# Two decoder layers on one core: weight parts moved into the common pool of slices, latent scores as three rounded products, c loaded as one row

## The chip, the core and the metric

The kernel runs on one core of one Trainium2 chip. The time is the device time in microseconds (us) of one launch. Engines: PE is TensorE (matrix products and transposes), ACT is ScalarE, DVE is VectorE, POOL is GpSimd, SP is SyncE, which here issues all transfers. SBUF is the on-chip memory of 128 partitions, PSUM the accumulators that PE writes, in banks of 128x512 fp32.

## The reference

One sequence of 512 tokens of width 1024 passes two layers of three sub-layers each. Every sub-layer is wrapped alike, and the six inner functions are, in order: feed-forward, latent attention, feed-forward, feed-forward, dilated attention, feed-forward.

```python
def sandwich(x, fn, pre_g, post_g, shift, scale, gate, res_w):
    hn = rmsnorm(x, pre_g) * (1 + scale[:, None, :]) + shift[:, None, :]
    y = rmsnorm(fn(hn), post_g)
    return x + res_w * gate[:, None, :] * y

def swiglu(h, w_gate, w_up, w_down):
    return (jax.nn.silu(h @ w_gate) * (h @ w_up)) @ w_down
```

shift, scale and gate are rows of `silu(c) @ w_mod[i] + b_mod[i]`, with c one row of 1024 numbers. Latent attention (16 heads) projects h to 384 query and 256 key-value numbers and a shared rotary key of 32, normalizes them, expands them to queries and keys of 64 + 32 and values of 64 per head, and takes causal softmax attention. Dilated attention (16 heads of 64) projects h to nine blocks (query, key and value for three dilations), scores each query against a window of keys with a bias, and mixes the three results by their log-sums. All data is fp32; D_MODEL is 1024 and D_FF 2816.

## The kernel before

**Products.** A dense product is `mm3` (L141 to L146): both operands are held as a rounded part and a rest, in the type fp32r, and three products are summed in one bank: high by high (L143), high by low (L144) and low by high (L145). For w the two operand pairs are `w[0]`, `w[1]`; either the weights or the activations stand on the side that is loaded into the array. The scores of latent attention are the exception: one fp32 product of 96 rows (L847), for block i of 128 queries against the n = (i + 1)·128 columns of keys that the mask can leave, so 128, 256, 384 or 512.

**Weights.** `weights` (L123) fetches a 128x1024 block (512 KB) into a slot of the tag `raw` (RAW = 5 slots, L120), ACT writes its high part in one instruction (L128, tag `whi`), and DVE writes the low part in two halves (L130, tag `wlo`). `whi` and `wlo` have SLOTS = 6 slots of their own in the pool `ring`. Only the first two weights after each change of sub-layer are taken by `weights_sliced` and the class `Sliced` (L53 to L75, splits in L68 and L72): their parts lie in slices of 128x512.

**Slices.** The pool `sl` has SLICES = 44 slots of 128x512, all with the tag `s` (method `s`). From it come h, the partial sums y, the feed-forward's products g in two parts, latents, queries, keys, values, the dilated projections and their outputs, tables and biases. The slots of one tag are handed out in the order in which the program asks for them: the k-th request takes the slot that the request 44 before it leaves. Where an instruction lies in an engine's queue is set when the program is built, by a scheduler that keeps to such orders; on the chip each engine runs its queue strictly in order.

**Feed-forward** (`Ffn`). D_FF is cut into 22 units of 128, in groups of 5, 6, 5 and 6 (GROUPS). Of a unit, `gate_up_mm` sums 48 products of 128x512, 24 in a gate bank and 24 in an up bank, from two 128x1024 weights. `gate_up_out` (L540 to L557) then takes silu of the gate bank (ACT, L552), times the up bank (DVE, L554), the high part of the result g (ACT, L555) and its low part (DVE, L557). After a group, `down` multiplies g with the group's `w_down` blocks (one 128x1024 weight for each unit) in four tiles of 128 tokens and two halves of 512 columns, and `y_part` adds the bank to y. The last group's down products are the sub-layer's tail; during it the next sub-layer's input is normalized, transposed (`turn`) and modulated, and its first units are taken in halves of 256 tokens (`head`: three units of a feed-forward, six tiles of an attention). The first feed-forward starts four units together (START) in `start`, while x arrives.

**Latent attention** (`Mla`, from L685). After six tiles of `mla_in`, `rest` projects keys (`key`), queries (`query`), rotary queries (`rope`) and values (`value`), each when the table BESIDE says so, beside the attention of 8 pairs of heads in four blocks each (`attend`: scores on PE, masking and minimum on DVE L850, exp on ACT L853, transposes L875, products with the values).

**Dilated attention** (`Dil`, from L928). For each of 8 pairs of heads nine tiles are projected (`tile`: one 128x1024 weight, 24 products, a copy on ACT at L1040). Beside the tiles n = 0 to 8 of the next pair run the present pair's parts: at n = 0 to 3 the scores (PE L1075, DVE L1088), after the last of them `tops` (DVE L1120, L1121), which passes minima through DRAM by several transfers; at n = 4 `exps`, 24 exponentials on ACT (L1140) whose sums go through DRAM again (`norm`, L1159), then `norm_out` (DVE L1167 to L1169), which sends 1/sum through DRAM (L1170, L1173); at n = 6 to 8 transposes (L1195), copies (L1199) and products with the values (L1220).

**Start** (`start`, from L322). c is broadcast to 128 partitions by a transfer of 512 KB into `cs` (L379), silu is applied in place, and the rows of x are normalized (`rise`) and transposed (L370). `mod_fold` multiplies a 128x1024 block of `w_mod` with cs and sums each partition (DVE L165), then adds the bias (L168).

Of the kernel before, what the change touches and what calls it, by code (L numbers as in the profile page):

```python
# [14 lines left out]
P = 128  # L15
# [10 lines left out]
SLICES = 44  # L26
SLOTS = 6
# [16 lines left out]
class Halves:  # L44
    def __init__(self, parts):
        self.parts = [x.rearrange("p (k c) -> p k c", c=P) for x in parts]
# [6 lines left out]
class Sliced:  # L53


    def __init__(self, t, src):
        self.t, self.src = t, src
        self.raw = t.ring.tile([P, CH], F32, tag="raw", name="raw", bufs=RAW)
        self.out = [[t.s(F32R), t.s(F32R)] for _ in range(2)]

    def at(self, j):
        return slice(j * SEQ, (j + 1) * SEQ)

    def fetch(self, j):
        self.t.nc.sync.dma_start(self.raw[:, self.at(j)], self.src[:, self.at(j)])

    def top(self, j):
        self.t.nc.scalar.activation(self.out[0][j], self.raw[:, self.at(j)], AF.Copy)  # L68

    def low(self, j):  # L70
        hi, lo = self.out
        self.t.nc.vector.tensor_tensor(lo[j], self.raw[:, self.at(j)], f(hi[j]), ALU.subtract)  # L72
# [5 lines left out]
class Trunk:  # L78
    def __init__(self, ctx, tc, a):
# [3 lines left out]
        self.ring = ctx.enter_context(tc.tile_pool(name="ring", bufs=SLOTS))  # L83
# [39 lines left out]
    def weights(self, src, flat=False):  # L123
        raw = self.load(src)
        n = src.shape[-1]
        hi = self.ring.tile([P, CH], F32R, tag="whi", name="whi")[:, :n]
        lo = self.ring.tile([P, CH], F32R, tag="wlo", name="wlo")[:, :n]
        self.nc.scalar.activation(hi, raw, AF.Copy)  # L128
        for r in (slice(0, n // 2), slice(n // 2, n)):
            self.nc.vector.tensor_tensor(lo[:, r], raw[:, r], f(hi[:, r]), ALU.subtract)  # L130
        return [t if flat else t.rearrange("p (k c) -> p k c", c=P) for t in (hi, lo)]

    def weights_sliced(self, src):
        w = Sliced(self, src)
        for j in range(2):
            w.fetch(j)
            w.top(j)
            w.low(j)
        return w.parts()
# [19 lines left out]
    def mod(self, l, n, k):  # L159
        self.mod_fold(l, n, k, self.load(self.a["w_mod"][l, n, k]))  # L160

    def mod_fold(self, l, n, k, raw):
# [5 lines left out]
        self.mod_out(l, n, k, t, lambda out, b: nc.vector.tensor_tensor(out, t[:, 0:1], b, ALU.add))  # L168
# [163 lines left out]
    def start(self, sub):  # L332
# [19 lines left out]
        def rise(i):  # L352
# [10 lines left out]
            r = self.scale_of(ss)  # L363
            nc.vector.tensor_scalar(t[0], x[0], r, None, ALU.mult)
# [14 lines left out]
        nc.sync.dma_start(self.cs, self.a["c"].broadcast_to([P, D]))  # L379
        stream(0)  # L380
        stream(1)
        nc.sync.dma_start(self.small, self.a["small"])
        raw = [self.load(self.a["w_mod"][*mods[0], 0])]
        stream(2)
        raw.append(self.load(self.a["w_mod"][*mods[1], 0]))
        stream(3)
        w = [Sliced(self, self.a["w_gu"][sub.l, sub.s, 0, g]) for g in range(2)]
        sub.w[0] = [x.parts() for x in w]
        for j in range(2):
            for x in w:  # L390
                x.fetch(j)
# [3 lines left out]
        with self.tc.manual_schedule(engines={ACT, DVE}):  # L395
            nc.scalar.activation(self.cs, self.cs, AF.Silu)
            self.new_h()
            rise(0)
            rise(1)
            self.mod_fold(*mods[0], 0, raw[0])  # L400
            rise(2)
            self.mod_fold(*mods[1], 0, raw[1])
# [11 lines left out]
            for x in w:  # L414
                x.top(1)
                x.low(1)
# [3 lines left out]
        for n, kind in sorted([(n, 1) for n in range(1, START)] + [(n, 0) for n in range(1, KT)]):  # L420
            if kind:
                sub.gate_up_load(n)
# [83 lines left out]
class Ffn:  # L506
# [11 lines left out]
    def gate_up_load(self, ft, sliced=False):  # L518
        t = self.t
        make = t.weights_sliced if sliced else t.weights  # L520
        self.w[ft] = [make(t.a["w_gu"][self.l, self.s, ft, g]) for g in range(2)]

    def prepare(self):
        self.gate_up_load(0, True)
# [39 lines left out]
    def products(self, b, q, i, d, js):  # L564
        m = GROUPS[q][1]
        for j in js:
# [3 lines left out]
                [x[:, d * SEQ : (d + 1) * SEQ] for x in self.wd[q][j]],  # L570
# [4 lines left out]
    def down(self, q, i):  # L575
# [3 lines left out]
        if q not in self.wd:  # L579
            self.wd[q] = [  # L580
                t.weights(t.a["w_down"][self.l, self.s, at + j], flat=True) for j in range(m)
# [49 lines left out]
class Mixer:  # L631
# [5 lines left out]
    def out_weights(self, j):  # L637
        t = self.t
        if j not in self.wo:
            self.wo[j] = t.weights(t.a[self.w_o][j], flat=True)  # L640

    def products(self, b, i, d, js):
        t = self.t
        for j in js:
# [4 lines left out]
                [x[:, d * SEQ : (d + 1) * SEQ] for x in self.wo[j]],  # L649
# [35 lines left out]
class Mla(Mixer):  # L685
# [37 lines left out]
    def prepare(self):  # L723
        self.w = {u: self.t.weights_sliced(self.t.a["mla_in"][u]) for u in range(2)}
# [31 lines left out]
    def value(self, j, e):  # L756
        t = self.t
        if not self.wv:
            self.wv += [t.weights(t.a["mla_v"][k], flat=True) for k in range(2)]
        b = t.bank()  # L760
        for k in range(2):
            ls = [x[:, j * P : (j + 1) * P] for x in self.latn[k]]
            t.mm3(b, ls, [x[:, e * SEQ : (e + 1) * SEQ] for x in self.wv[k]], k == 0, k == 1)
# [8 lines left out]

    def key(self, g, p):
        t, nc = self.t, self.t.nc
        b = self.project(self.weight(g, 0), 2 * p, (0, 1))
        k = self.k[2 * g + p] = [t.s() for _ in range(2)]
        nc.scalar.activation(k[0][0:64], b[0:64], AF.Copy)
        nc.vector.tensor_copy(k[1][0:64], b[64:128])
        for y in k:
            nc.gpsimd.tensor_scalar(y[64:96], self.lat[2][64:96], 1.0, 0.0, ALU.mult, ALU.add)  # L780

    def query(self, g, p):
        nc = self.t.nc
        b = self.project(self.weight(g, 1), 3 * p, (3, 4, 5))
# [616 lines left out]
```

## Time and profile before

| | us |
|---|---|
| median of 3 runs | 2277.34 |
| lowest, highest | 2276.07, 2277.81 |
| the profiled execution's own time | 2277.64 |
| its span in the trace | 2275.9 |
| PE busy | 2241.0 |
| DVE busy | 1203.6 |
| ACT busy | 861.4 |
| POOL busy | 106.1 |

The time of a run is the span plus about 1.7 us around it (2277.64 against 2275.9). A row of the profile names the line, engine, operation, output and input of a group of instructions. In a window's row stand its bounds, its length, the busy time of PE, weight loads, DVE, ACT and POOL with the number of instructions behind each, the clock granted to PE as a share of full speed, the share of busy DMA and GB/s. A row of the timeline has the start in us from the begin of the span, the time taken and, in brackets, the idle time of the engine before it and what ended that. Matrix products overlap: the distance between two starts is what one costs, and the printed duration includes the part that lies under the next.

### The profile page before, as it was taken

What the parts mean: (1) busy time and instruction counts of PE and PEld (TensorE: products, weight loads), DVE (VectorE), ACT (ScalarE), POOL (GpSimd) and SP (SyncE); (2) the same over time, 40 slices, a digit from 0 to 9 for tenths busy, and PEclk for the clock granted to TensorE, in tenths of its full rate; (3) what the DMA queues carried; (4) which work ended last, traced back from release to release, by engine and by line L of the source; (5) the groups of instructions that cost most, each with busy time, mean ns of one, the idle gap of its engine ahead of it and who ended that gap; (6) DMA issues with size and microseconds to landing.
All of it is one profiled execution on the core that took longest, in us unless ns stands there. A gap on an engine that the chain in (4) does not pass through costs nothing. (4 is left out here: it accounts for less than half of the span.)

```text
span 2275.9 us, 30179 instructions
## 1 busy us (share of the span) xinstructions
PE 2241.0 (98%) x11418; PEld 1853.5 (81%) x11418; DVE 1203.6 (53%) x2711; ACT 861.4 (38%) x1751; POOL 106.1 (5%) x143
## 2 busy tenths in 40 slices
PE   6999999999999999999999999999999999999998
PEld 5888888877898888898888888777878878888887
DVE  7666566677665366474554473344334367243344
ACT  4432135577633132353222352444344345332232
POOL 0000001210110000020000010000000002000000
PEclk9999999999999999999999999999999999999999
DMA  8575662211255365344653523333333332242231
GB/s 311 162 251 183 186 231 69 99 47 56 70 172 184 93 208 176 107 140 123 192 175 114 155 93 105 80 95 88 83 89 80 96 79 79 75 130 98 79 111 37
DMA packets 121366, 284.56 MB, mean 125 GB/s; under 512 B 44145, under 2 KB 48516, under 8 KB 121220
## 3 DMA queue, kind: packets, MB, share of 16 engines
q1 hardware_dynamic: 121220, 282.63, 40.5%
q8 instruction: 89, 1.46, 0.3%
q14 instruction: 57, 0.47, 0.1%
HBM read 280.19 MB, written 2.39 MB: 124 GB/s over the span
## 5 line engine op out<-in xcount | busy, mean ns | idle before, releaser
L143 PE MATMUL mm<-s,whi 128*128 128x512 f32 (+1 forms) x2116 | 797.8, 378 | 3.7 <-ACT whi L128 2.5
L144 PE MATMUL mm<-s,whi 128*128 128x512 f32 (+1 forms) x2116 | 792.2, 374 | 0.0
L145 PE MATMUL mm<-s,wlo 128*128 128x512 f32 (+1 forms) x2116 | 791.5, 374 | 0.0
L128 ACT ACTIVATE whi<-raw 128x1024 fp32r<-128x1024 f32 (+1 forms) x356 | 369.7, 1053 | 973.2 <-PE mm L144 441.8
L130 DVE TENSOR_TENSOR wlo<-raw,whi 128x512 fp32r<-128x512 f32 (+1 forms) x712 | 466.0, 693 | 409.9 <-ACT whi L128 401.7
L143 PEld LDWEIGHTS mm<-s,whi 128*128 128x128 f32 x2116 | 399.3, 189 | 84.4 <-issue 7.0
L145 PEld LDWEIGHTS mm<-s,wlo 128*128 128x128 f32 x2116 | 399.6, 189 | 70.9
L144 PEld LDWEIGHTS mm<-s,whi 128*128 128x128 f32 x2116 | 399.5, 189 | 67.8
L143 PE MATMUL mm<-whi,s 128*128 128x512 f32 x848 | 332.4, 392 | 2.0 <-ACT s L679 1.3
L144 PE MATMUL mm<-wlo,s 128*128 128x512 f32 x848 | 330.4, 390 | 0.0
L145 PE MATMUL mm<-whi,s 128*128 128x512 f32 x848 | 330.1, 389 | 0.0
L165 DVE CUSTOM_DVE_ANT_0 raw<-raw,cs 128x1024 f32<-128x1024 f32 x130 | 160.1, 1236 | 108.5 <-DMA raw<-w_mod 107.9
L143 PEld LDWEIGHTS mm<-whi,s 128*128 128x128 f32 x848 | 159.2, 188 | 36.6 <-issue 2.5
L145 PEld LDWEIGHTS mm<-whi,s 128*128 128x128 f32 x848 | 159.2, 188 | 33.4 <-issue 0.3
L144 PEld LDWEIGHTS mm<-wlo,s 128*128 128x128 f32 x848 | 159.2, 188 | 32.6 <-issue 0.3
L554 DVE TENSOR_TENSOR gg<-silu,mm 128x512 f32<-128x512 f32 (+1 forms) x95 | 60.4, 635 | 172.2 <-PE mm L145 168.8
L444 DVE TENSOR_TENSOR s<-mm,s 128x512 f32<-128x512 f32 x112 | 76.5, 689 | 124.8 <-PE mm L145 124.7
L314 POOL TENSOR_TENSOR mv<-mv,mhalf 128x1 f32<-128x1 f32 x48 | 35.9, 750 | 1498.9 <-DVE mv L313 1496.4
L555 ACT ACTIVATE s<-gg 128x512 fp32r<-128x512 f32 (+1 forms) x97 | 57.4, 591 | 53.3 <-DVE gg L554 53.2
L552 ACT ACTIVATE silu<-mm 128x512 f32<-128x512 f32 (+1 forms) x95 | 51.4, 543 | 30.6 <-PE mm L145 30.5
L1040 ACT ACTIVATE s<-mm 128x512 f32<-128x512 f32 (+3 forms) x156 | 46.2, 374 | 34.8 <-PE mm L145 34.8
L448 ACT ACTIVATE s<-mm 128x512 f32<-128x512 f32 x40 | 23.8, 595 | 85.8 <-PE mm L145 85.5
(165 smaller groups left out, 1738.1 us busy)
## 6 DMA issues: line engine op xcount, KB each, us to landing
raw<-w_gu SPq DMA_DIRECT2D x168, 512.0 KB, 4.4
raw<-w_mod SPq DMA_DIRECT2D x130, 512.0 KB, 4.7
raw<-w_down SPq DMA_DIRECT2D x88, 512.0 KB, 4.3
raw<-dil_in SPq DMA_DIRECT2D x70, 512.0 KB, 3.6
s<-w_mod SPq DMA_DIRECT2D x28, 256.0 KB, 6.6
raw<-w_gu SPq DMA_DIRECT2D x16, 256.0 KB, 3.2
raw<-mla_o SPq DMA_DIRECT2D x8, 512.0 KB, 4.7
raw<-dil_o SPq DMA_DIRECT2D x8, 512.0 KB, 3.7
```

The lines of the kernel that those rows point to most:

```text
L128: self.nc.scalar.activation(hi, raw, AF.Copy)
L130: self.nc.vector.tensor_tensor(lo[:, r], raw[:, r], f(hi[:, r]), ALU.subtract)
L143: mm(out, w[0], m[0], start=first, stop=False)
L144: mm(out, w[0], m[1], start=False, stop=False)
L145: mm(out, w[1], m[0], start=False, stop=last)
L165: nc.vector.tensor_tensor_reduce(raw, raw, self.cs, 1.0, 0.0, ALU.mult, ALU.add, accum_out=t[:, 0:1])
L314: nc.gpsimd.tensor_tensor(v[:, 1:2], v[:, 0:1], self.mhalf[:, 0:1], ALU.pow)
L444: nc.vector.tensor_tensor(y, b, y, ALU.add)
L552: nc.scalar.activation(s, banks[0], AF.Silu)
L554: nc.vector.tensor_tensor(v, s, banks[1], ALU.mult)
L555: nc.scalar.activation(ghi, v, AF.Copy)
L1040: nc.scalar.activation(out, src, AF.Copy)
```

## The change

**One pool for weights too.** SLOTS and the tags `whi` and `wlo` are gone; SLICES is 68 instead of 44, which takes the room that became free (6 slots of two 128x1024 parts are 24 slices). The class `Sliced` is now `Weights`, and every weight's parts are four slices of the tag `s` (two high, two low), requested when the program creates the weight. A high part is two instructions of 128x512 on ACT (now L75), the low part two on DVE (now L79). The raw block is still fetched by one transfer, of 512 KB, into one of 5 slots (now L68 in the list of transfers).

**Scores of latent attention.** Queries and keys are split into high and low parts (`part_rows`: three ACT and two DVE instructions of 64x512 on one bank), the shared rotary key and the rotary queries too (`turned_parts`, `rope`), and the scores are three fp32r products.

**Start.** c comes as one row of 4 KB, is spread over the partitions by two products with a row of ones, and silu reads it from PSUM. The two first blocks of `w_mod` are fetched ahead of the second and third tile of x, `small` after x. `mod_fold` is cut into `mod_dot` and `mod_sum`. The second halves of the first two weights are fetched and split later (at n == 2).

```diff
-SLICES = 44
-SLOTS = 6
+SLICES = 68
...
-class Sliced:
+class Weights:
     def __init__(self, t, src):
-        self.t, self.src = t, src
+        self.t, self.src, self.n = t, src, src.shape[-1]
         self.raw = t.ring.tile([P, CH], F32, tag="raw", name="raw", bufs=RAW)
         self.out = [[t.s(F32R), t.s(F32R)] for _ in range(2)]
...
     def top(self, j):
-        self.t.nc.scalar.activation(self.out[0][j], self.raw[:, self.at(j)], AF.Copy)
+        self.t.nc.scalar.activation(self.both(j)[0], self.raw[:, self.at(j)], AF.Copy)
     def low(self, j):
-        hi, lo = self.out
-        self.t.nc.vector.tensor_tensor(lo[j], self.raw[:, self.at(j)], f(hi[j]), ALU.subtract)
+        hi, lo = self.both(j)
+        self.t.nc.vector.tensor_tensor(lo, self.raw[:, self.at(j)], f(hi), ALU.subtract)
...
-        self.ring = ctx.enter_context(tc.tile_pool(name="ring", bufs=SLOTS))
+        self.ring = ctx.enter_context(tc.tile_pool(name="ring", bufs=RAW))
...
-    def weights(self, src, flat=False):
-        raw = self.load(src)
-        n = src.shape[-1]
-        hi = self.ring.tile([P, CH], F32R, tag="whi", name="whi")[:, :n]
-        lo = self.ring.tile([P, CH], F32R, tag="wlo", name="wlo")[:, :n]
-        self.nc.scalar.activation(hi, raw, AF.Copy)
-        for r in (slice(0, n // 2), slice(n // 2, n)):
-            self.nc.vector.tensor_tensor(lo[:, r], raw[:, r], f(hi[:, r]), ALU.subtract)
-        return [t if flat else t.rearrange("p (k c) -> p k c", c=P) for t in (hi, lo)]
-
-    def weights_sliced(self, src):
-        w = Sliced(self, src)
+    def weights(self, src):
+        w = Weights(self, src)
+        w.fetch(0, 1)
         for j in range(2):
-            w.fetch(j)
             w.top(j)
             w.low(j)
         return w.parts()
...
-        nc.sync.dma_start(self.cs, self.a["c"].broadcast_to([P, D]))
+        row = self.tmp.tile([P, D], F32, tag="gb", name="gb", bufs=1)[0:1]
+        nc.sync.dma_start(row, self.a["c"])
         stream(0)
+        raw = [self.load(self.a["w_mod"][*mods[0], 0])]
         stream(1)
+        raw.append(self.load(self.a["w_mod"][*mods[1], 0]))
+        stream(2)
+        stream(3)
         nc.sync.dma_start(self.small, self.a["small"])
...
+        for d in range(2):
+            nc.tensor.matmul(cb[d], one, row[:, d * SEQ :][:, :SEQ], start=True, stop=True)
...
-            nc.scalar.activation(self.cs, self.cs, AF.Silu)
+            for d in range(2):
+                nc.scalar.activation(self.cs[:, d * SEQ :][:, :SEQ], cb[d], AF.Silu)
...
+    def part_rows(self, b):
+        t, nc = self.t, self.t.nc
+        hi, lo, u = [t.s(F32R), t.s(F32R)], [t.s(F32R), t.s(F32R)], t.s()
+        up, down, r = b[0:64], b[64:128], slice(0, 64)
+        nc.scalar.activation(hi[0][r], up, AF.Copy)
+        nc.scalar.activation(hi[1][r], down, AF.Copy)
+        nc.scalar.activation(u[r], down, AF.Copy)
+        nc.vector.tensor_tensor(lo[0][r], up, f(hi[0][r]), ALU.subtract)
+        nc.vector.tensor_tensor(lo[1][r], u[r], f(hi[1][r]), ALU.subtract)
+        return [hi, lo]
...
     def key(self, g, p):
...
-        nc.scalar.activation(k[0][0:64], b[0:64], AF.Copy)
-        nc.vector.tensor_copy(k[1][0:64], b[64:128])
...
+        k = self.k[2 * g + p] = self.part_rows(self.project(self.weight(g, 0), 2 * p, (0, 1)))
+        for ys, src in zip(k, self.turned):
+            for y in ys:
+                nc.gpsimd.tensor_scalar(y[64:96], f(src[64:96]), 1.0, 0.0, ALU.mult, ALU.add)
...
-                nc.tensor.matmul(s, q[e][0:96, i * P : n], k[e][0:96, :n], start=True, stop=True)
+                qs, ks = [x[e][0:96, i * P : n] for x in q], [x[e][0:96, :n] for x in k]
+                for j, (a, b) in enumerate(((0, 0), (0, 1), (1, 0))):
+                    nc.tensor.matmul(s, qs[a], ks[b], start=j == 0, stop=j == 2)
```

The order of the instructions moves at every change of unit or tile. Three places stand for the rest. In the names, the number is that of the tile, in the order in which the program creates them.

ACT before, first feed-forward, second group of units: silu_1003 reads the gate bank mm_937 of one unit, s_1001 is its g; raw_1027 and higher belong to later units (the weights of the unit of mm_1027 are raw_1029 and raw_1036, and those of mm_1118 are raw_1120 and raw_1127; all four high parts stand above these rows).

```order
L552 ACTIVATE silu_1003<-mm_937 128x512
L128 ACTIVATE whi_1209<-raw_1207 128x1024
L128 ACTIVATE whi_1216<-raw_1214 128x1024
L555 ACTIVATE s_1001<-gg_1005 128x512
L128 ACTIVATE whi_1296<-raw_1294 128x1024
L552 ACTIVATE silu_1093<-mm_1027 128x512
L128 ACTIVATE whi_1303<-raw_1301 128x1024
L555 ACTIVATE s_1091<-gg_1095 128x512
L128 ACTIVATE whi_1385<-raw_1383 128x1024
L552 ACTIVATE silu_1184<-mm_1118 128x512
```

Each unit's silu has one or two high parts of the unit three places on beside it.

ACT of the change at the same place: the unit of bank mm_1080 has the weights raw_1082 and raw_1092, the next one raw_1179 and raw_1189.

```order
L563 ACTIVATE silu_1056<-mm_984 128x512
L566 ACTIVATE s_1054<-gg_1058 128x512
L75 ACTIVATE s_1083<-raw_1082 128x512
L75 ACTIVATE s_1084<-raw_1082 128x512
L75 ACTIVATE s_1093<-raw_1092 128x512
L75 ACTIVATE s_1094<-raw_1092 128x512
L563 ACTIVATE silu_1152<-mm_1080 128x512
L566 ACTIVATE s_1150<-gg_1154 128x512
L75 ACTIVATE s_1180<-raw_1179 128x512
L75 ACTIVATE s_1181<-raw_1179 128x512
```

The splits that stand behind a unit's silu are now those of the very next unit, and they stand behind the high part of the former unit's g too, which asked for its slices first.

ACT before in dilated attention, around the exponentials of one pair (L1040 is the copy of a projected tile):

```order
L128 ACTIVATE whi<-raw 128x1024
L1040 ACTIVATE s<-mm 128x512
L1140 ACTIVATE u,dz<-u,y_13274 128x128 x8
L128 ACTIVATE whi<-raw 128x1024
L1140 ACTIVATE sq,dz<-sq,y_13274 128x128
L1140 ACTIVATE sq,dz<-sq,y_13274 128x256
L1140 ACTIVATE sq,dz<-sq,y_13274 128x128
L1140 ACTIVATE sq,dz<-sq,y_13274 128x256 x5
L1140 ACTIVATE u,dz<-u,y_13274 128x128 x8
L128 ACTIVATE whi<-raw 128x1024 x2
L1040 ACTIVATE s<-mm 128x128 x8
```

One high part stands between the exponentials and two behind them, all for tiles that are still some places off.

ACT of the change there (L1070 is the copy, L1170 the exponentials):

```order
L75 ACTIVATE s<-raw 128x512 x2
L1070 ACTIVATE s<-mm 128x512
L1170 ACTIVATE u,dz<-u,y_13701 128x128 x8
L1170 ACTIVATE sq,dz<-sq,y_13701 128x128
L1170 ACTIVATE sq,dz<-sq,y_13701 128x256
L1170 ACTIVATE sq,dz<-sq,y_13701 128x128
L1170 ACTIVATE sq,dz<-sq,y_13701 128x256 x5
L1170 ACTIVATE u,dz<-u,y_13701 128x128 x8
L75 ACTIVATE s<-raw 128x512 x2
L1070 ACTIVATE s<-mm 128x128 x4
L75 ACTIVATE s<-raw 128x512 x2
```

The high part of tile n = 4 now stands behind all 24 exponentials, and each later one behind the copy of the tile before it.

DVE before in the same stretch (L1120, L1121 are `tops`, L1199 copies of transposes, L1167 the first step of `norm_out`, L130 the low parts of weights):

```order
L1120 TENSOR_TENSOR y_13274<-x_13272 128x8
L1121 TENSOR_TENSOR y_13274<-y_13274,dm 128x8
L130 TENSOR_TENSOR wlo<-raw,whi 128x512 x2
L1199 COPY silu<-aux 128x512 x2
L130 TENSOR_TENSOR wlo<-raw,whi 128x512 x2
L1199 COPY gg<-aux 128x384 x2
L130 TENSOR_TENSOR wlo<-raw,whi 128x512 x2
L1167 TENSOR_TENSOR w_13350<-x_13347 128x4x2
```

A pair of low parts follows each step.

DVE of the change there (L1150 and L1151 are now `tops`, L1229 the copies, L1197 to L1199 `norm_out`, L79 the low parts):

```order
L1150 TENSOR_TENSOR y_14276<-x_14274 128x8
L1151 TENSOR_TENSOR y_14276<-y_14276,dm 128x8
L1229 COPY silu<-aux 128x512
L1229 COPY gg<-aux 128x384
L1229 COPY silu<-aux 128x512
L1229 COPY gg<-aux 128x384
L1221 STREAM_TRANSPOSE gg<-u 128x512 x2
L1197 TENSOR_TENSOR w_14355<-x_14352 128x4x2
L1198 TENSOR_TENSOR w_14355<-w_14355,dz 128x4x2
L1199 RECIPROCAL w_14355<-w_14355 128x8
L79 TENSOR_TENSOR s<-raw,s 128x512 x8
```

The low parts that stood between these steps, for tiles still to come, now stand in one row behind the last of them, the reciprocal.

107 lines of the change are left out of this document (59 added, 48 removed).

## The prediction

> **What bounds the kernel now.** I read the page first: how much of the span has a busy PE, and at which clock.
>
> ```profile
> span 2275.9 us, 30179 instructions
> PE 2241.0 (98%) x11418; PEld 1853.5 (81%) x11418; DVE 1203.6 (53%) x2711; ACT 861.4 (38%) x1751; POOL 106.1 (5%) x143
> PEclk9999999999999999999999999999999999999999
> GB/s 311 162 251 183 186 231 69 99 47 56 70 172 184 93 208 176 107 140 123 192 175 114 155 93 105 80 95 88 83 89 80 96 79 79 75 130 98 79 111 37
> ```
>
> PE idles 2275.9 - 2241.0 = 34.9 us in all, at full clock. The time is the number of products times their distance; anything that lets PE wait adds to it, and little is left to gain but cheaper products and the start. ACT and DVE have time to spare. The waits show how that time is used; a row gives the total in us, how many there were and the longest.
>
> ```profile
> ACT whi L128 <- PE mm L144: 441.8, 140, 6.3
> ```
>
> Among SP's transfers (the DMA queue's own waits) the largest group is this:
>
> ```profile
> SPq L120 <- DVE wlo L130: 1240.8, 321, 36.2
> ```
>
> Both say that the weights run ahead: ACT waits 140 times for PE to free an old high part before it may write a new one, and the transfers wait for a free raw slot. PE never waits here for a split, because a ring of six lies between. That ring is what the change takes apart.
>
> Next the timeline at a change of unit in the first feed-forward, PE, DVE and ACT: the last product of an up bank (155.00), what follows it, and a later product of the next unit.
>
> ```profile
> 155.00 0.39 PE L145 MATMUL mm<-s,wlo 128*128 128x512 f32 x1
> 155.50 0.69 DVE L554 TENSOR_TENSOR gg<-silu,mm 128x512 f32<-128x512 f32 x1 [3.30 <-PE mm L145]
> 156.22 0.63 ACT L555 ACTIVATE s<-gg 128x512 fp32r<-128x512 f32 x1
> 156.91 0.68 DVE L557 TENSOR_TENSOR s<-gg,s 128x512 fp32r<-128x512 f32 x1
> 158.40 0.39 PE L145 MATMUL mm<-s,wlo 128*128 128x512 f32 x1
> ```
>
> From 155.00 to 158.40 lie 15 products: 3.40 / 15 = 0.227 us each. The next unit's products run while gg, g and its rest are made; PE does not notice the boundary. The durations of splits and copies come from the groups (busy us, mean ns of one):
>
> ```profile
> L68 ACT ACTIVATE s<-raw 128x512 fp32r<-128x512 f32 x24 | 13.4, 619 | 0.0
> L72 DVE TENSOR_TENSOR s<-raw,s 128x512 fp32r<-128x512 f32 x24 | 15.4, 685 | 0.6 <-ACT s L68 0.6
> L1040 ACT ACTIVATE s<-mm 128x512 f32<-128x512 f32 x44 | 26.2, 600 | 28.1 <-PE mm L145 28.1
> L787 ACT ACTIVATE s<-mm 64x512 f32<-64x512 f32 x16 | 9.4, 586 | 2.4 <-PE mm L145 2.3
> ```
>
> **The pool: a wait at nearly every boundary.** Slices go out in program order, so in the new queue of ACT the high parts of unit k+1 stand behind silu and the high part of g of unit k, and on DVE the low parts behind gg and g's rest (the first place shown of the order). Neither can be done before unit k's up bank is. So the cover is gone, and PE waits for this chain, counted from the start of the last product: gg starts at 0.50 and g at 1.22 (rows 155.50, 156.22), g ends at 1.85; consecutive ACT splits overlap by 0.06 (13.4 / 24 = 0.56 each where one takes 0.62), so the split runs from 1.79 to 2.41, and PE starts near 2.42 instead of 0.227: 2.19 us idle. The third product needs the low part: DVE does g's rest from 1.91 (156.91) to 2.59, then the split of 0.69, 0.04 sooner for the overlap (15.4 / 24 = 0.64), to 3.24; the product would have started at 2.42 + 2 x 0.227 = 2.87. That is 0.37 more: **2.56 us a boundary**.
>
> How many: the order of ACT gives, for each of the four feed-forwards, 19 places where the splits for the next work stand directly behind the last g: unit 4, the first weights of the four groups' down products, and units 6 to 10, 12 to 15 and 17 to 21. (Units 11 and 16 are covered by the down products before them.) 4 x 19 x 2.56 = 195. Six heads in halves, 2.4 each, 14; unit 5 behind the first copies of y, 1.8 each, 7. At the down products the weights also come too slowly: the first pass over them uses 3 x 0.227 = 0.68 us for each weight, while DVE needs 2 x 0.64 = 1.28 for its two low halves, so 0.6 x 3 or x 4 weights, 2.1 us in the mean, 16 times: 34. Together **250 us** (205 to 290; a `w_mod` product of DVE may stand in front of gg and make a gap longer, a free DVE shorter).
>
> **The clock.** Three stretches of 3.40 us in which PE waited (length, PE busy, weight loads, DVE, ACT, POOL, granted clock), each with the stretch behind it:
>
> ```profile
> 447.30:450.70 3.40, 1.98 (x10) 1.31 (x9) 1.61 (x6) 2.80 (x5) 2.52 (x4) 1.00 0.37 113
> 450.70:454.10 3.40, 3.40 (x10) 2.69 (x10) 1.32 (x6) 3.08 (x10) 0.16 (x1) 0.56 0.11 43
> 1901.40:1904.80 3.40, 2.16 (x10) 1.25 (x9) 3.34 (x8) 3.38 (x9) 0.55 (x1) 1.00 0.00 0
> 1904.80:1908.20 3.40, 3.40 (x19) 3.40 (x19) 3.29 (x7) 3.40 (x9) 1.44 (x2) 0.56 0.58 172
> 1880.90:1884.30 3.40, 2.08 (x9) 1.42 (x8) 1.72 (x3) 1.68 (x3) 0.00 (x0) 1.00 0.01 3
> 1884.30:1887.70 3.40, 3.40 (x16) 2.80 (x15) 3.22 (x7) 1.34 (x4) 0.31 (x1) 1.00 0.00 0
> ```
>
> A stretch with 1.24 to 1.42 us idle was twice followed by one at 0.56, once not: the threshold lies near 1.3 us idle in such a window. A half-clock window costs 3.40 x (1 - 0.56) = 1.5 us. A gap of 2.4 us idle falls under the threshold in both windows that it touches only when it is split almost evenly; I take 0.8 of the gaps as throttled. 70 gaps x 0.8 x 1.5 = 84, and 0.5 for each of the 16 at the down products, where PE waits for weights anyway: **92 us** (0 to 120). The Trainium skill ("TensorE: Matmul & The Clock Gate", "Why this matters for your kernels") says that throughput falls after PE-idle gaps of more than about 3 us, one whole idle window. By that rule none of the 2.56 us gaps would be throttled; the trace does not agree, since the rows 447.30 and 1901.40 had over half of the window busy. I go by the rows.
>
> **Dilated attention.** The pair at 1552 us, SP, ACT and DVE, from the last score (t = 0 is 1552.7):
>
> ```profile
> 1552.64 0.08 DVE L1088 DVE_READ_ACCUMULATOR2_ANT dm<- 128x1 f32 x1
> 1561.77 0.37 SPq L1123 DMA_DIRECT2D y<-t  x1
> 1570.22 0.39 ACT L1140 ACTIVATE u<-u,y 128x128 f32<-128x128 f32 x1
> 1570.72 1.71 SPq L1107 DMA_DIRECT2D z<-dz  x4
> 1573.04 0.35 SPq L120 DMA_DIRECT2D raw<-dil_in  x1
> 1573.61 0.38 SPq L1159 DMA_DIRECT2D x<-z  x1
> 1577.79 0.17 DVE L1167 TENSOR_TENSOR w<-x 128x8 f32<-128x8 f32 x1 [2.22 <-DMA x<-z]
> 1578.21 0.20 DVE L1169 RECIPROCAL w<-w 128x8 f32<-128x8 f32 x1
> 1580.25 1.09 SPq L1173 DMA_DIRECT2D s<-d  x2
> ```
>
> This chain lies off PE's path now: transfers of minima, 24 exponentials to +17.9, transfers of sums, the reciprocal at +25.7. In the new order the high part of tile n = 4 stands behind the last exponential and its low part behind the reciprocal. The raw transfer that stood ahead of x<-z (1573.04) moves behind, so the chain ends about 1 to 2 us sooner, at +24; the split ends at +24.7. PE has until then only tile n = 3 (24 x 0.227 = 5.4 us, to about +3.5) and 14 transposes and 8 small products, some 22 records at 0.15 (from the row 461.62 below), 3.4 us: 24.7 - 3.5 - 3.4 = 17.8, say 18 us for each of 7 pairs, **126**, and one half-clock window each, 7 x 1.5 = **11**. At the other boundaries of a pair PE waits for the copy (0.60), the high part (0.62) and two semaphores' time behind the last product, 1.8 to 2.1 where nothing else is queued, 1.0 to 1.3 where scores or transposes are: 7 x 1.5 = 10.5 a pair. SP's transfers of the weights from n = 5 on stand behind s<-d (1580.25, t = +27.6 to +28.6); they land 3.6 us later (raw<-dil_in in the page's list), about +32, when tile 4 ends near +30: 2.5 more. 7 x 13 = **91**. Heads, first tiles and the end: **20**. Sum 248 (170 to 300).
>
> ```profile
> raw<-dil_in SPq DMA_DIRECT2D x70, 512.0 KB, 3.6
> ```
>
> **Latent attention.** The stretch of the attention, in the same columns:
>
> ```profile
> 448.00:570.00 122.00, 120.73 (x745) 88.21 (x746) 87.76 (x272) 93.97 (x227) 16.54 (x23) 0.99 0.18 53
> ```
>
> `part_rows` and the rotary parts add about 32 ACT instructions (24 of 64x512, 8 of 32x512) and 5 splits; at 0.59 (L787) 19 + 3 = 22 us, some 18 in this stretch, where ACT has 94 of 122 us already. 94 + 18 = 112 fits barely, and the splits of later weights now wait behind copies of values: 15 us (0 to 30). Before it, values and the first weights stand behind the keys' chain: 15; heads 10; the end 5. **45** (20 to 75). The scores (PE, four records for two products):
>
> ```profile
> 457.51 1.88 PE L847 MATMUL mm<-s 96*128 96x512 f32 x4
> 459.22 0.60 PE L875 MATMUL aux<-ident,u 128*128 128x128 f32 x4
> 461.62 0.61 PE L847 MATMUL mm<-s 96*128 96x128 f32 x4
> ```
>
> Two fp32 products of 512 columns take 459.22 - 457.51 = 1.71, 0.855 each; three of fp32r 3 x 0.227 = 0.681: -0.174 each. If the narrower ones (768 columns more) gain in proportion it is -0.435 a head, -7 over 16; if the small ones cost as much per product as fp32 (461.62: at most 0.15 a record), they lose what the wide gain: +1. I take **-4**.
>
> **The start** (SP, DVE, PE):
>
> ```profile
> 0.74 0.39 SPq L379 DMA_DIRECT2D cs<-c  x1
> 14.01 1.22 DVE L165 CUSTOM_DVE_ANT_0 raw<-raw,cs 128x1024 f32<-128x1024 f32 x1
> 15.55 0.69 DVE L358 CUSTOM_DVE_ANT_0 s<-x 128x512 f32<-128x512 f32 x1
> 19.75 0.79 PE L143 MATMUL mm<-s 128*128 128x512 f32 x1
> ```
>
> 512 KB of broadcast leave the front of the queue (1.7 us at the 311 GB/s of the page's first slice), and the second product of w_mod no longer stands 14.01 to 15.55 in front of the last tile: 1.5. **-3** (-6 to 0).
>
> **The sum.** 2277.6 (the profiled execution, 0.3 above the median) + 250 + 92 + 126 + 11 + 91 + 20 + 45 - 4 - 3 = 2905.6, so **2905 us**.
>
> **The rivals.**
>
> *The clock holds* (0.17). A gap under 2.6 us never throttles, the two half-clock stretches had another cause. Then 92 + 11 go: 2905 - 103 = 2802. For it: 1880.90 did not throttle with 1.32 idle. Against: the other two did with as much.
>
> *The gaps are covered* (0.04), which ends faster. The place is the first high part of the next unit behind g (L75 behind L566): if on the chip the raw data and slices let PE's next products start no later than about 0.3 us after an up bank, as at 155.00 to 155.23 now, no boundary costs anything, and 2277.6 - 4 - 3 = 2271 is left. It decides at one point: whether that split starts before the last product of the former unit. For it speaks that ACT is 62% idle; against it, that a queue runs in order and g needs the full bank.
>
> *More than the chain* (0.10): raw transfers and `w_mod` products of DVE (1.22 each) stand in front of gg or the low parts at most boundaries: 80 x 1.2 = 96 more, about 3001.
>
> **The numbers.** The forecast has 0.67, the rest of 0.02 lies between. The low end, 2740, is the full-clock case with some half of what the low bounds of the waits allow (45, 78 and 25: 62 of 148). The high end, 2990, is the forecast with some half of what the upper bounds allow (40, 28 for the clock, 52, 30: 85 of 150). What a measurement can tell from no change is 0.2%, 4.6 us: faster 0.04, same 0.01, slower 0.95.
>
> **What the new profile would show.** PE near 80% busy (2241 and the half-clock time, some 100, against 2904), some 80 gaps of 2 to 3 us in the feed-forwards ended by ACT's or DVE's splits (L75, L79), seven of about 18 us in dilated attention ended by L79, a granted clock below 0.97. Wrong would be: L75 ahead of the silu in time, or gaps under 1 us. A mean clock of 0.99 would point to the first rival.

## The result, and the profile after

The changed kernel takes 2855.85 us (median of 4 runs, 2850.31 to 2859.16) against 2277.57 for the kernel before on the same chip (4 runs): 1.254 times the time, 95% interval 1.2525 to 1.2555. The forecast was 2905, with a range of 2740 to 2990. The profiled execution took 2859.16 us with a span of 2857.4.

The page of the changed kernel:

```profile
span 2857.4 us, 30524 instructions
PE 2442.5 (85%) x11486; PEld 1920.2 (67%) x11486; DVE 1221.5 (43%) x2741; ACT 912.5 (32%) x2145; POOL 119.0 (4%) x167
```

PE idles 2857.4 - 2442.5 = 414.9 us instead of 34.9, and its busy time grew by 201 us though only 68 instructions came in: the same products count for longer. The largest three waits of PE in the changed kernel, and one of DVE:

```profile
PE mm L140 <- ACT s L75: 256.0, 121, 13.8
PE mm L142 <- DVE s L79: 57.0, 29, 6.0
PE aux L1225 <- ACT sq L1170: 45.6, 8, 7.3
...
DVE raw L162 <- DMA raw<-w_mod: 308.2, 98, 15.0
```

PE now waits for the splits of weights (L75, L79), which it did not before. One boundary in the last feed-forward, from the last product of an up bank, in the timeline of the changed kernel:

```profile
2745.21 0.39 PE L142 MATMUL mm<-s 128*128 128x512 f32 x1
2745.71 0.69 DVE L565 TENSOR_TENSOR gg<-silu,mm 128x512 f32<-128x512 f32 x1 [10.26 <-PE mm L142]
2746.43 0.63 ACT L566 ACTIVATE s<-gg 128x512 fp32r<-128x512 f32 x1 [5.63 <-DVE gg L565]
2746.96 2.18 ACT L75 ACTIVATE s<-raw 128x512 fp32r<-128x512 f32 x4
2747.63 0.50 PE L140 MATMUL mm<-s 128*128 128x512 f32 x1 [2.03 <-ACT s L75]
2747.70 2.49 DVE L79 TENSOR_TENSOR s<-raw,s 128x512 fp32r<-128x512 f32 x4
2747.96 0.40 PE L141 MATMUL mm<-s 128*128 128x512 f32 x1
2748.44 0.50 PE L142 MATMUL mm<-s 128*128 128x512 f32 x1
```

Row by row it is the chain of the prediction, counted from the start of the last product: gg starts 0.50 later, g 1.22, the next unit's first product 2.42, its third product 3.23 (the one that needs the low part). ACT's four splits run as one row behind g, though their raw data had been requested 30 us earlier (SP's last two loads before them are issued from 2715.68 on): they wait for nothing but their place in the queue.

Next the windows by stage (length, PE busy, weight loads, DVE, ACT, POOL, granted clock). The stages are the first feed-forward, latent attention, two feed-forwards, dilated attention and the last feed-forward. The kernel before:

```profile
0.00:400.30 400.30, 382.26 (x1698) 315.18 (x1699) 258.01 (x558) 140.52 (x211) 15.16 (x23) 1.00 0.60 199
400.30:624.50 224.20, 221.43 (x1397) 177.31 (x1396) 154.00 (x406) 150.44 (x347) 33.69 (x44) 0.99 0.21 66
624.50:987.20 362.70, 362.00 (x1735) 305.14 (x1734) 199.29 (x383) 117.94 (x181) 16.39 (x17) 1.00 0.47 151
987.20:1353.20 366.00, 365.31 (x1762) 308.45 (x1761) 197.63 (x381) 119.53 (x183) 16.39 (x18) 1.00 0.48 146
1353.20:1915.60 562.40, 556.97 (x3176) 450.84 (x3175) 258.41 (x770) 233.75 (x690) 14.09 (x29) 1.00 0.35 90
1915.60:2275.90 360.30, 353.05 (x1664) 296.55 (x1662) 136.28 (x218) 99.24 (x142) 10.42 (x12) 1.00 0.28 88
```

The same six stages of the changed kernel:

```profile
0.00:495.10 495.10, 414.33 (x1677) 323.27 (x1678) 257.96 (x552) 138.31 (x267) 14.53 (x22) 0.94 0.49 160
495.10:748.90 253.80, 228.01 (x1458) 189.51 (x1456) 169.23 (x432) 172.25 (x407) 53.19 (x68) 0.96 0.17 54
748.90:1207.60 458.70, 392.77 (x1740) 316.27 (x1739) 201.01 (x387) 123.86 (x245) 14.52 (x18) 0.94 0.39 120
1207.60:1660.60 453.00, 392.57 (x1762) 316.92 (x1761) 196.70 (x381) 124.64 (x246) 14.14 (x18) 0.95 0.38 118
1660.60:2426.10 765.50, 636.40 (x3166) 469.73 (x3165) 256.44 (x762) 242.14 (x768) 12.33 (x28) 0.93 0.24 65
2426.10:2857.40 431.30, 378.41 (x1694) 304.46 (x1692) 140.11 (x230) 111.27 (x216) 10.32 (x13) 0.97 0.24 77
```

The four feed-forward stages grew by 94.8 + 96.0 + 87.0 + 71.0 = 348.8 us, dilated attention by 203.1, latent attention by 29.6. In each, the idle time is the length less PE's busy time. Feed-forwards: 233 us more idle. Dilated attention: 129.1 - 5.4 = 124 more idle.

What the clock costs can't be read from the granted clock of a stage alone, because the clock is also halved while PE waits. Behind the longest gap, which ended at 1022.29:

```profile
1013.25:1022.29 9.04, 0.00 (x0) 0.00 (x0) 3.83 (x8) 1.20 (x3) 0.00 (x0) 0.50 0.27 76
1022.29:1026.90 4.61, 4.61 (x11) 3.53 (x12) 2.56 (x5) 1.51 (x3) 0.00 (x0) 0.50 0.62 211
```

The first 9.04 us at half clock cost nothing, since PE had nothing to do; the 4.61 after them cost half of their length. Summed over all half-clock stretches of the four feed-forwards, PE is busy in 133 of 172 us, so the clock costs 133 / 2 = 66 us there. The other 348.8 - 66 = 283 us are the waits: 233 of idle time and some 50 at the edges of the gaps. There the end of the last product, 0.16 us under no other product, counts as busy, and the first product takes 0.33 until the next starts (2747.63 to 2747.96) instead of 0.227.

### The profile page after: what moved, and what is told of

Its sections match the earlier page's. It is cut to its first block, busy times and chain, and to the rows that moved or that the text cites. A ratio compares the mean times of both kernels' runs of the same rounds, so it can differ in the third digit from the quotient of the medians.

```text
span 2857.4 us, 30524 instructions
## 1 busy us (share of the span) xinstructions
PE 2442.5 (85%) x11486; PEld 1920.2 (67%) x11486; DVE 1221.5 (43%) x2741; ACT 912.5 (32%) x2145; POOL 119.0 (4%) x167
## 4 chain that ended last, share of the span: by engine, by line
PE 59%; DVE 12%; DMA 12%; ACT 9%; issue 5%; POOL 1%; SPq 1%; DVEq 0%; POOLq 0%; ACTq 0%
PE mm L142 19%; PE mm L140 19%; PE mm L141 18%; DMA raw<-w_mod 9%; DVE s L79 4%; DVE raw L162 2%; DVE gg L565 2%; ACT s L75 2%; ACT s L566 1%; ACT sq L1170 1%; ACT u L1170 1%; ACT s L1070 1%; POOL mv L315 1%; PE mm L1105 1%; DMA x<-m 1%
## 5 line engine op out<-in xcount | busy, mean ns | idle before, releaser
L140 PE MATMUL mm<-s 128*128 128x512 f32 (+1 forms) x3140 | 1223.3, 393 | 263.4 <-ACT s L75 256.0
L142 PE MATMUL mm<-s 128*128 128x512 f32 (+1 forms) x3140 | 1219.0, 390 | 60.1 <-DVE s L79 57.0
L141 PE MATMUL mm<-s 128*128 128x512 f32 (+1 forms) x3140 | 1207.6, 386 | 4.0 <-DVE s L304 1.8
L140 PEld LDWEIGHTS mm<-s 128*128 128x128 f32 x3140 | 616.0, 196 | 424.4 <-ACT s L75 312.2
L142 PEld LDWEIGHTS mm<-s 128*128 128x128 f32 x3140 | 615.0, 196 | 214.5 <-DVE s L79 108.0
L141 PEld LDWEIGHTS mm<-s 128*128 128x128 f32 x3140 | 615.4, 196 | 121.5 <-DVE s L79 5.3
L79 DVE TENSOR_TENSOR s<-raw,s 128x512 fp32r<-128x512 f32 x736 | 467.8, 686 | 333.1 <-ACT s L75 332.8
L75 ACT ACTIVATE s<-raw 128x512 fp32r<-128x512 f32 x736 | 406.6, 618 | 22.4 <-DMA raw<-w_gu 15.6
L1070 ACT ACTIVATE s<-mm 128x512 f32<-128x512 f32 (+3 forms) x156 | 48.9, 370 | 469.1 <-PE mm L142 469.1
L568 DVE TENSOR_TENSOR s<-gg,s 128x512 fp32r<-128x512 f32 x79 | 54.7, 692 | 44.2 <-ACT s L566 44.1
L1225 PE MATMUL aux<-ident,sq 128*128 128x128 f32 x112 | 30.6, 418 | 45.8 <-ACT sq L1170 45.6
L1225 PEld LDWEIGHTS aux<-ident,sq 128*128 128x128 f32 x112 | 16.2, 191 | 63.5 <-ACT sq L1170 57.4
L1170 ACT ACTIVATE u<-u,y 128x128 f32<-128x128 f32 x128 | 49.4, 387 | 19.9 <-DVE y L1151 19.9
L1229 DVE COPY silu<-aux 128x512 f32<-128x512 f32 x32 | 21.3, 686 | 77.7 <-PE aux L1225 76.0
L460 ACT ACTIVATE s<-mm 128x512 f32<-128x512 f32 x40 | 23.9, 598 | 87.4 <-PE mm L142 87.1
L1105 PE MATMUL mm<-s 64*128 64x128 f32 (+1 forms) x384 | 46.4, 324 | 0.0
```

Source lines behind the costliest of these rows:

```text
L75: self.t.nc.scalar.activation(self.both(j)[0], self.raw[:, self.at(j)], AF.Copy)
L79: self.t.nc.vector.tensor_tensor(lo, self.raw[:, self.at(j)], f(hi), ALU.subtract)
L140: mm(out, w[0], m[0], start=first, stop=False)
L141: mm(out, w[0], m[1], start=False, stop=False)
L142: mm(out, w[1], m[0], start=False, stop=last)
L1070: nc.scalar.activation(out, src, AF.Copy)
```

## The experiments

**The weights' parts in slots of their own.** Whole change, but for the pool:

```diff
-SLICES = 68
+SLICES = 44
+OWN = 24
-        self.out = [[t.s(F32R), t.s(F32R)] for _ in range(2)]
+        self.out = [[t.part(), t.part()] for _ in range(2)]
+    def part(self):
+        return self.ring.tile([P, SEQ], F32R, tag="part", name="part", bufs=OWN)
```

> The whole change, but the weights' parts take 24 slots of 128x512 of their own (a tag of their own) and the common pool has 44 again. Theory (the order of requests in one pool makes the waits, nothing else): the splits run ahead again, PE's idle time falls from 415 us to under 50, the clock is back above 0.99, and the time is 2265 to 2295 us. Rival (the splits of 512 columns, the three products of the scores and the added copies cost time by themselves): PE keeps waiting for L75 and L79 and the time stays above 2400 us.

2291.1 us, 1.0063 times the kernel before (1.0049 to 1.0076). Its page:

```profile
span 2289.3 us, 30934 instructions
PE 2244.9 (98%) x11486; PEld 1862.6 (81%) x11486; DVE 1234.8 (54%) x2741; ACT 945.5 (41%) x2145; POOL 119.2 (5%) x167
```

44.4 us of idle PE are left of 414.9. The same instructions on the same memory, with two tags instead of one, are 565 us faster; ACT is even 33 us busier than in the whole change. The rival falls. What the remaining 14 us above the kernel before are was not followed up; 9 of them lie in the second and third feed-forward (737.8 us against 728.7).

**The pool alone**, on the kernel before (its scores and its start kept; edit: the hunks of the change that concern SLICES, SLOTS, `Weights` and `weights`).

> The kernel before with the pool part of the change alone: one pool of 68 slices for weights too; fp32 scores and the old start. Theory: it has nearly the whole loss, 2825 to 2855 us, with 2.03 us of idle PE at a feed-forward's boundary. Rival (latent attention's added ACT and DVE work and the start carry a good part of it): under 2800 us.

2857.25 us, 1.2543 times (1.2526 to 1.2561): the whole loss, and 2 us above the top of what was expected. In sum the other two parts add nothing to it. PE's waits in this kernel repeat those of the change:

```profile
PE mm L140 <- ACT s L75: 251.6, 120, 10.8
PE mm L142 <- DVE s L79: 55.2, 27, 5.9
```

**The scores alone** (`part_rows`, `turned_parts`, three products), with the ring.

> The kernel before with the three rounded products in the scores alone, the weights in their ring. Theory: the products gain about 4 us on PE and the added ACT and DVE work hides behind PE, so 2270 to 2280 us. Rival (ACT, 94 us busy of 122 before, becomes the bound with some 18 us more and PE waits for queries and keys): 2285 to 2305 us.

2279.73 us, 1.0012 times (1.0004 to 1.0021): at the upper end of the theory's range, but 3 us slower than the kernel before instead of faster, so not all of the added work hides. The products did gain: from start to start the 128 fp32 records of the kernel before take 36.1 us in all, the 192 fp32r ones here 34.0. But at the first score PE waits 3.8 us. The rows of ACT before the first score, which starts at 452.04:

```profile
449.00 0.63 ACT L818 ACTIVATE s<-s 128x512 fp32r<-128x512 f32 x1 [3.38 <-DVE s L816]
449.66 0.59 ACT L778 ACTIVATE s<-mm 64x512 fp32r<-64x512 f32 x1
450.26 0.59 ACT L779 ACTIVATE s<-mm 64x512 fp32r<-64x512 f32 x1
450.76 0.58 ACT L780 ACTIVATE s<-mm 64x512 f32<-64x512 f32 x1
451.36 1.28 ACT L798 ACTIVATE s<-s 32x512 fp32r<-32x512 f32 x2
```

ACT's added copies hide later, but here they are the chain to the first score.

**The start alone**, with the ring and fp32 scores.

> The kernel before with the new start alone. Theory from the trace of the changed kernel (first main product at 19.24 us instead of 19.75, then 2.9 us of idle PE): no difference that can be measured, 2274 to 2280 us. Rival (the prediction's step): 3 us faster, 2271 to 2275 us.

2274.78 us, 0.9989 times (0.9981 to 0.9998): 1.9 us faster than 2276.67, where the two expected ranges overlap, so it does not decide between them. It is the one version that is faster than both kernels.

**The weights requested ahead, in the one pool.** First in the feed-forwards only:

```diff
     def head(self, ft, lo, hi):
         banks = [self.t.bank()[:, : hi - lo] for g in range(2)]
         self.gate_up_mm(ft, lo, hi, banks, range(KT))
+        self.ask((2, ft, None))
         self.gate_up_out(ft, lo, hi, banks)
```

`ask` creates the next four weights in order of use, if they don't exist yet; `start` and `down` call it too.

> The whole change with its one pool of 68 slices, but in the feed-forwards the program requests the slices of the next four weights before it requests those of a unit's g, and those of the next group behind the down products' weights. Theory (the order of the requests, not the sharing of the pool, puts the splits behind silu and g): the four feed-forward stages fall back to about their time before (395, 367, 366 and 354 us from 493, 459, 453 and 424), the others stay: 2490 to 2530 us. Rival (a shared pool gives slices back too late whatever the order): above 2650 us.

2530.83 us, 1.1114 times (1.1097 to 1.113), 0.8 above the expected band. The second feed-forward, 458.7 us in the change:

```profile
669.90:1031.40 361.50, 360.89 (x1720) 302.94 (x1719) 197.48 (x381) 120.48 (x240) 13.78 (x17) 1.00 0.49 151
```

0.6 us of idle PE, full clock: the time before, from one shared pool. Then in dilated attention too (`tile` creates the weights of the next four tiles before it takes its output slice):

> As the run before, and in dilated attention the weights of the next four tiles are requested before a tile's own output slice. Theory: dilated attention, 766 us in the change and 562 before, comes down to 565 to 600, so 2300 to 2350 us in all; the rest is latent attention. Rival (the exponentials' chain itself holds PE there, whatever the weights do): 2450 us or more.

2333.36 us, 1.0248 times (1.0233 to 1.0264). Dilated attention in this kernel:

```profile
1403.20:1969.70 566.50, 553.87 (x3141) 447.70 (x3140) 252.36 (x759) 237.29 (x764) 12.69 (x28) 0.99 0.31 86
```

765.5 became 566.5 us, 4 above the kernel before. So the chain of exponentials and small transfers costs PE next to nothing once weights are split ahead of it, and sharing one pool did not by itself make the loss. Of the 56 us that remain, 35 lie in latent attention (259.6 against 224.2), whose weights were not requested ahead.

**Fewer slices**: `SLICES = 60` in the whole change.

> The whole change with 60 slices instead of 68. Theory (the order of the requests decides, the pool has slices to spare): 2840 to 2870 us, no difference. Rival (the pool is too small, and each slice less makes the waits longer): 2890 us or more.

2855.15 us (2 runs), 1.2538 times (1.2513 to 1.2563), as with 68. Eight slices were spare, so the number of slices did not make the loss either.

**Filling the gaps.** Behind each full unit of the feed-forwards of the whole change:

```diff
         self.gate_up_mm(ft, lo, hi, banks, range(KT))
+        if hi - lo == SEQ:
+            b = self.t.bank("aux")
+            for k in range(8):
+                self.t.nc.tensor.matmul(
+                    b, self.w[ft][1][0][:, k, :], self.t.h[0][k], start=True, stop=True
+                )
         self.gate_up_out(ft, lo, hi, banks)
```

> The whole change with eight products of 128x512 more on PE behind each full unit of the feed-forwards, whose results nobody reads, 1.8 us at full clock in a gap of 2.2. Theory (the gaps cost a second time, because PE's clock is halved for a window behind each): the fillers lie in time that PE waits anyway, the granted clock of the feed-forwards (0.94 to 0.97 by stage) goes to 0.98 or more, and 60 to 95 us are saved: 2760 to 2800 us. Rival (the gap alone costs, the clock is no matter, or is halved for another reason): 2850 us or more.

2817.54 us, 1.2375 times (1.2354 to 1.2396): 600 instructions more and 38 us less. The second and third feed-forward of this kernel:

```profile
742.20:1185.80 443.60, 415.69 (x1892) 336.38 (x1891) 201.35 (x387) 123.67 (x245) 14.78 (x18) 0.98 0.39 124
1185.80:1625.40 439.60, 413.89 (x1914) 335.16 (x1914) 197.52 (x381) 124.69 (x246) 14.93 (x18) 0.99 0.38 121
```

The clock goes from 0.94 and 0.95 to 0.98 and 0.99, and the stages from 458.7 and 453.0 to 443.6 and 439.6. So the gaps do cost a second time through the clock. The size that was expected, 60 to 95, was missed, because the clock cost less than the 93 us that the stages' lengths, times what their granted clock lacks of 1.00, suggest. Counted as above, by PE's busy time at half clock, it cost 66 us in the change and costs 22 here (half of 43.5). The clock so gives back 44 us, and the four stages are 45 shorter, which accounts for the gain.

**Small packets.** In the changed kernel a gap of 13.83 us ended at 1022.29 (the longest of the first wait above). SP just before, then DVE:

```profile
995.98 0.38 SPq L221 DMA_DIRECT2D row<-mG  x1
999.51 16.59 SPq L127 DMA_DIRECT2D raw<-w_mod  x2
```

```profile
1014.51 1.23 DVE L162 CUSTOM_DVE_ANT_0 raw<-raw,cs 128x1024 f32<-128x1024 f32 x1 [15.02 <-DMA raw<-w_mod]
```

A block of `w_mod` issued at 999.5 landed 15 us later (the median of its kind is 4.4), and DVE's gg, which PE's next weights wait for, stands behind its product. Ahead of it went row<-mG, 1024 packets of 4 bytes. The edit makes them 128 of 32. With it the gates arrive in another order, so this kernel leaves out their right order and serves for timing alone:

```diff
-                nc.sync.dma_start(row.rearrange("(k p) -> p k", p=P), self.G[:, l, sub])
+                nc.sync.dma_start(row.rearrange("(p k) -> p k", p=P), self.G[:, l, sub])
```

> The whole change, but each of the six transfers that write a gate row to DRAM sends 128 packets of 32 bytes instead of 1024 of 4 bytes; the 1024 gates so arrive in another order, a part of the computation that is changed here. Theory (512 KB loads that follow those small packets land 12 to 15 us after their issue instead of 4, and the change has no weights ahead to cover that): the gaps of 6 to 14 us in the feed-forwards go, 2815 to 2835 us. Rival (these gaps come from raw slots that are freed late, whatever the small packets do): 2850 us or more.

2820.21 us, 1.239 times (1.2371 to 1.2409), 35.6 less than the change. Row<-mG itself lands after 1.4 to 3.5 us instead of 10 to 14, and no load of that run takes over 8.5 us instead of 15; the longest wait of PE for a split falls to 7.9:

```profile
PE mm L140 <- ACT s L75: 229.4, 122, 7.9
```

**A version to beat both.** The ring of six for the weights, the new start, the three products, and in latent attention:

```diff
+        self.query_rows(0, 0)
         self.rope(0)
-        self.query(0, 0)
+        self.query_rope(0, 0)
         self.value(2, 0)
```

> The kernel before with its ring of six for the weights, and with the new start and the three rounded products of the scores; in latent attention the first query's rows are split ahead of its rotary part, since in the run with the scores alone PE waited 3.8 us for that chain at the first score. Theory: the start gives 2 us, the score products 2, and the shorter chain most of what the scores alone lost: 2269 to 2275 us, faster than the kernel before by 0.1 to 0.3%. Rival (the chain at the first score stays, the rotary addition on DVE being its last step): 2276 to 2280 us.

2281.42 us, 1.0019 times (1.001 to 1.0027): a miss, above both ranges. The gap at the first score is still 4.1 us, and the rotary copy ends it, not the rows. Latent attention takes 228.9 us against 224.2 before, which is more than the start gains. The start alone stays the best.

## Why the prediction was right, and where it was off

The sum of 2905.6 lies 46 us above the profiled execution of the change (2859.16). Dilated attention was put 45 too high and latent attention 11; the feed-forwards with the start came out 10 above their 339 (250 + 92 - 3), with two errors that cancel in part. Of the signs, the gaps and the granted clock (0.947, below 0.97) came as forecast; PE is 85% busy instead of near 80.

**What decides.** Right: place in the queue, set by the order of requests. Shown from both sides: with slots of their own, or with earlier requests in the same pool, the same splits are early again; with the pool alone the loss is whole.

**The boundary, 2.56 us.** Right to a few hundredths: first product 2.42 after the last (2745.21 to 2747.63), third 3.23 (to 2748.44) against 3.24 forecast. Unit to unit took 13.55 us where the clock held, 10.88 of products (48 x 0.227) and 2.67.

**The feed-forwards' waits, 250.** 283 measured, idle time and edges together, so 33 too low. The step that failed is "at the down products the weights also come too slowly", 34 us. The change at one such place, the first down products of the last feed-forward:

```profile
2491.47 1.03 PE L140 MATMUL mm<-s 128*128 128x512 f32 x2 [2.06 <-ACT s L75]
2491.54 6.11 DVE L79 TENSOR_TENSOR s<-raw,s 128x512 fp32r<-128x512 f32 x10
2498.36 1.28 ACT L460 ACTIVATE s<-mm 128x512 f32<-128x512 f32 x2 [2.25 <-PE mm L142]
```

The copies of both halves of the columns (L460) stand together, 6.9 us after the first product, the time of 30 products: PE takes the two halves side by side. A weight so feeds 6 products, 1.36 us, DVE's 1.28 keeps up, and PE has no further wait there. In place of that term came gaps that are longer than the chain, above all behind late `w_mod` blocks: without the small packets the kernel was 36 us faster. I had them only as the heavier rival in another form (1.2 at most boundaries). What else makes up the 33 was not taken apart.

**The clock, 92 + 11.** In the feed-forwards 66 measured instead of 92: the term was mis-sized, and that it makes up for most of the missing waits is luck. The threshold was the wrong step. The 1.3 us idle came from stretches of 3.40 us that I had cut where the gaps lay; the clock of this trace changes on a fixed grid of 3.41 us. Two gaps of the last feed-forward on that grid, each with the window behind it:

```profile
2532.18:2535.59 3.41, 1.39 (x5) 0.87 (x6) 2.69 (x5) 2.67 (x5) 0.00 (x0) 1.00 0.00 0
2535.59:2539.01 3.42, 3.42 (x10) 2.65 (x9) 1.09 (x2) 0.05 (x1) 0.00 (x0) 0.50 0.70 186
2743.81:2747.22 3.41, 1.79 (x8) 1.13 (x7) 0.82 (x2) 0.79 (x2) 0.00 (x0) 1.00 0.00 0
2747.22:2750.63 3.41, 2.92 (x12) 2.13 (x13) 2.97 (x5) 1.92 (x4) 0.00 (x0) 1.00 0.20 36
```

PE waits 2.03 us in both. Where all but 1.39 us of a window were idle, the next window ran at half clock; where the edge of the grid cut the gap and left 1.79 busy, it did not. The whole trace of the change has 52 full-clock windows with less than 1.45 us of busy PE, and all 52 were followed by half clock; of the 687 with more, 3 were. So a gap is throttled by where it falls on the grid: in the feed-forwards 35 half-clock stretches stand against 84 gaps of about 2.03 us or more, 0.4 of them instead of 0.8. Units of 13.55 us keep their place for long, being close to four windows (13.65), which is why they come in series at 1.00. The first rival, a clock that holds at such gaps, is out. The Trainium skill ("TensorE: Matmul & The Clock Gate", "Why this matters for your kernels") puts the limit at idle gaps of more than about 3 us; the trace does not agree, since the window that was followed by half clock had 2.02 us idle.

**Dilated attention, 248.** Measured 203, and the split differs. A pair of the changed kernel, DVE's last score, PE's transposes, ACT's last exponential, DVE's chain end and PE's return:

```profile
1838.95 0.08 DVE L1118 DVE_READ_ACCUMULATOR2_ANT dm<- 128x1 f32 x1
1849.17 3.53 PE L1225 MATMUL aux<-ident,sq 128*128 128x128 f32 x12 [6.49 <-ACT sq L1170]
1855.05 0.39 ACT L1170 ACTIVATE u<-u,y 128x128 f32<-128x128 f32 x1
1860.50 0.20 DVE L1199 RECIPROCAL w<-w 128x8 f32<-128x8 f32 x1
1861.32 0.80 PE L142 MATMUL mm<-s 128*128 128x512 f32 x1 [3.64 <-DVE s L79]
```

From the last score (1839.03) the exponentials end at +16.4 and PE goes on at +22.3, not +24.7: with no splits and raw loads between them, they and the transfers run closer together than the pair that I read. PE was done with tile 3 at +3.6; of the 18.7 us until its return 6.5 and 3.6 are idle and 8.5 go into transposes, small products and two products of the next tile, for which I had 3.4. The time lost is 18.7 - 3.4, 15 instead of 18. The step that failed most is the other boundaries, "7 x 1.5 ... and 2.5 more": about 4.2 us of idle a pair (0.3 to 1.45 each) instead of 13. Beside scores, where I had charged 1.0 to 1.3, PE waits 0.3 to 0.4; why so little there was not tried.

The clock is halved twice in that pair, once behind each wait of the chain, and not behind the short waits:

```profile
1846.10:1856.34 10.24, 7.15 (x27) 3.64 (x28) 2.40 (x4) 10.06 (x47) 0.00 (x0) 0.50 0.07 2
1859.76:1866.58 6.82, 5.26 (x12) 4.13 (x13) 1.71 (x5) 0.00 (x0) 0.00 (x0) 0.50 0.39 83
```

The first stretch lies in time in which PE has to wait for the chain anyway. The second runs on behind PE's return and costs half of its 5.26; over the seven pairs that is 18 us instead of 11.

**Latent attention, 45 - 4.** 29.6 measured in sum. The pool alone makes 25.2 of them (249.4 against 224.2); in the ring the three products and their splits are +2.5 us of stage. Of the -4, the products gave 2.1: the 128-column ones cost as much each in fp32r as in fp32, 0.113 us against 0.112.

**The start, -3.** 1.9 by itself.

## What to carry to other kernels

A pool whose slots are handed out in program order ties the early work of one thing to the late work of another: a tag of its own, or a request placed earlier in the program, is what keeps prefetched work ahead, and here 60 slots did as well as 68. In the queue order of a new version, look first at how many units ahead of its use each preparation stands; "directly behind the last result" means that its whole chain lies open at every boundary. A gap on TensorE can be priced twice, as a wait and as a slower clock behind it; the clock's part is half of the time that PE is busy at half clock, not the mean clock times the length. That an engine is mostly idle (ACT at 32%) says nothing about either.

## What the runs showed that I had not expected

- Loads behind 1024 packets of 4 bytes land 12 to 15 us after their issue, in the kernel before too (13.8 us in the median of two blocks of `w_mod` issued at 229 us), where the weights ahead covered it. With 128 packets of 32 bytes none took over 8.5.
- Idle products can pay: eight unread products of 512 columns in each gap made the kernel 38 us faster, by what the clock gave back in the feed-forwards (44 of 45 us).
- Three fp32r products of 128 columns cost half as much again as one fp32 product (3 x 0.113 against two records of 0.112); at 512 columns they are cheaper, 3 x 0.233 against two records of 0.429.
